# Weight pieces cut by half the columns instead of by rows, with five buffers for their split halves instead of six

## The chip, the cores and the metric

The kernel runs on one core of a Trainium2 chip. The metric is the device time of one execution in microseconds (us). TensorE multiplies matrices (PE in the profile), VectorE (DVE), ScalarE (ACT) and GpSimd (POOL) work element by element, and SyncE (SP) issues most of the DMAs. Each engine takes its own instructions strictly in the order in which they were written into its queue, and waits for semaphores in between.

## The reference

Two layers act on 512 tokens of 1024 values, each as `h = h + mixer(rms_norm(h)) @ w_out`, with an inner width of 2048. A last RMS norm closes it.

```python
def pool_mixer(h, w_in, w_grp, scale, w_out):          # layer 0
    v, gate = jnp.split(h @ w_in, 2, axis=-1)
    p = multiscale_pool(v)                              # 4 groups of 512, windows 2, 4, 8, 16
    m = jnp.einsum('btgc,gcd->btgd', p, w_grp).reshape(B, T, D_INNER) * scale
    return (m * jax.nn.silu(gate)) @ w_out

def hgrn2_mixer(h, w_in, lb, norm_g, w_out):            # layer 1, 16 heads of 128
    q, fz, i, gate = jnp.split(h @ w_in, 4, axis=-1)
    ...                                                 # forget gates, per head: S_t = diag(f_t) S_{t-1} + k_t v_t^T
    o = hgrn2_chunk_scan(qc, kc, vc, bc)                # o_t = S_t^T q_t
    o = o * lax.rsqrt(jnp.mean(o * o, axis=-1, keepdims=True) + EPS) * norm_g
    return (o * jax.nn.silu(gate)) @ w_out
```

## The kernel before

Activations lie with the features on the partitions, as tiles of 128 x 512 tokens. All large products are made from three fp32r matmuls (`mm3`, L127 to L130): a weight or activation `x` is split into `hi` (rounded by ACT, L96) and `lo = x - hi` (by DVE, L97), and the product is hi·hi + hi·lo + lo·hi. One such matmul has 512 columns.

Weights come in pieces of 128 x 1024 values (512 KB). For each piece `piece` (L99) takes a buffer `wraw` (three of them) for the DMA on SP's queue and a buffer each of `whi` and `wlo` (`WB`, six of each), issues the DMA, the ACT cast and the DVE subtraction, all with raised priority so that the scheduler places them early in the engines' queues. A cast waits until PE has made its last use of the piece that had the buffer before.

A group is 512 of the 2048 inner columns, four blocks of 128 (`n` = 0 to 3). `load_in` brings the 1024 x 512 weights of a group in four pieces of 256 rows each, so that every block `n` needs all four pieces: `project` (L142) runs over the eight row blocks `k` for one `n`. `load_out` brings the 512 x 1024 output weights in four pieces of 128 rows.

Layer 1 works on four groups of four heads. For group 1 to 3, `prepare` makes the forget gates (`forget`: the weights `wf`, then `fz`, the sigmoids `s1` on ACT, `f` and `kk` on DVE), a chain of twelve products along the chunk on `f` (L557, L558) for each pair of heads, and then `queries` (weights `wq`, `q`). From `f` POOL makes `r` (L571), DVE takes the reciprocal of `r` (L572, four in a group), and q and k are scaled by it. Then `inputs` (weights `wi`) makes `v` with the weights as the moving side: each of its blocks needs all four pieces, one after the other, from the first block on. After that come the attention of four heads, gates and `add_out`, which adds the output product to `ht` (tokens on the partitions, four blocks `b`, two halves of the columns).

`finish` (L505) makes the last output product. For each token block `b` it makes half 0 and half 1, adds each to `ht` (DVE, L379), squares them (ACT, L514), and then makes the factor of the norm (`ms` on DVE, L516 and L517, the power on POOL, L519) and the two outputs `y` (DVE, L523), which ACT and SP send away.

Tile and a priority scheduler set the order in each engine's queue; nothing is ordered by hand beyond `tc.high_priority`.

Of the kernel before, what the change touches and what calls it, by code (L numbers as in the profile page):

```python
# [32 lines left out]
F32 = mybir.dt.float32  # L33
# [7 lines left out]
P = 128  # L41
D = 1024
T = 512
DI = 2048
# [7 lines left out]
WINDOWS = (2, 4, 8, 16)  # L52
RAW, WB = 3, 6
WARM = 10
# [12 lines left out]
def trunk(ctx: ExitStack, tc: tile.TileContext, xT, x_d, par, ident_d, causal_d, mask_d, fg_d, w0_in, w0_grp, w0_out, w1_in, w1_out, out):  # L67
# [31 lines left out]
    def piece(src, ahead=AHEAD):  # L99

        raw = wpool.tile([P, 2, GC], F32, name="wraw", tag="wraw", bufs=RAW)
        hi = wpool.tile([P, 2, GC], F32R, name="whi", tag="whi", bufs=WB)
        lo = wpool.tile([P, 2, GC], F32R, name="wlo", tag="wlo", bufs=WB)
        with tc.high_priority(ahead):
            nc.sync.dma_start(out=raw, in_=src)
            split(raw, hi, lo)
        return hi, lo

    def load_in(w, col=0, ahead=AHEAD):
# [6 lines left out]
        return out  # L116

    def load_out(w, g):

        out = []  # L120
        for i in range(GT):
            r = g * GC + i * P
            hi, lo = piece(w[r:r + P, :].rearrange("p (a b) -> p a b", a=2))
            out.append((hi.rearrange("p a b -> p (a b)"), lo.rearrange("p a b -> p (a b)")))
        return out
# [20 lines left out]
    def project(pieces, n, xs, at=None):  # L146


        if at:
            acc = pa.tile([P, T], F32, name="a", tag="a", bufs=4)  # L150
        else:
            acc = ps.tile([P, T], F32, name="mm", tag="mm", bufs=4)
        c = slice(n * P, (n + 1) * P)
        for k, ((wh, wl), (xh, xl)) in enumerate(zip(pieces, xs)):
            if at and k in at:
                at[k]()
            mm3(acc, wh[:, c], wl[:, c], xh, xl, k == 0, k == len(pieces) - 1)
        return acc
# [60 lines left out]
    def project_out(pieces, zs):  # L219
        for n in range(KD):  # L220
            acc = project(pieces, n, zs)
            nc.vector.tensor_tensor(out=h[n], in0=acc, in1=h[n], op=ALU.add)  # L222


    with tc.tile_pool(name="l0", bufs=1) as l0:
# [20 lines left out]
        accs = project4(pieces, xs, None)  # L246
        wg0 = load_in(w0_in, DI, AHEAD0)
        norm = []
# [13 lines left out]
        def values(g):  # L262
            vs = []
            wv = None if g == 0 else load_in(w0_in, g * GC)
# [24 lines left out]
        def gates0(g):  # L289
            wg = wg0 if g == 0 else load_in(w0_in, DI + g * GC)  # L290
            out = []
# [11 lines left out]
        def mixed(g, ps_, gates):  # L303
            wm = load_in(w0_grp[g])
            out = []
# [43 lines left out]
    def hgrn(ctx, general):  # L349
# [23 lines left out]
        def out_half(pieces, zs, b, half):  # L373

            acc = ps.tile([P, 512], F32, name="mm", tag="mm", bufs=4)
            t, c = slice(b * P, (b + 1) * P), slice(half * 512, (half + 1) * 512)
            for k, ((wh, wl), (zh, zl)) in enumerate(zip(pieces, zs)):
                mm3(acc, zh[:, t], zl[:, t], wh[:, c], wl[:, c], k == 0, k == len(pieces) - 1)
            nc.vector.tensor_tensor(out=ht[b][:, c], in0=acc, in1=ht[b][:, c], op=ALU.add)  # L379

        def add_out(pieces, zs):
            for b in range(TB):
                for half in range(2):
                    out_half(pieces, zs, b, half)
# [10 lines left out]
        def forget(g, store):  # L395
            wf = None if g == 0 else load_in(w1_in, DI + g * GC)
            fs, ks = [], []
# [13 lines left out]
        def queries(g):  # L411
            wq = load_in(w1_in, g * GC)
            qs = []
# [63 lines left out]
        def group(g, prepare, heads, zs):  # L477
# [6 lines left out]
            if first or last:  # L484
                wg = load_in(w1_in, 3 * DI + g * GC)
                gts = gates1(wg, (0, 1))
                ons = [attend(n) for n in range(GT)]
                gts += gates1(wg, (2, 3))
            else:
                add_out(load_out(w1_out, g - 1), zs)  # L490
                ons = [attend(n) for n in range(GT)]
                gts = gates1(load_in(w1_in, 3 * DI + g * GC), range(GT))
            if first:
# [9 lines left out]
        def finish(zs):  # L503
# [3 lines left out]
            for i in range(2):  # L507
                nc.scalar.dma_start(out=fg[i], in_=fg_d[:, i * 512:(i + 1) * 512])
            for b in range(TB):
                ss = l1.tile([P, 2], F32, name="ss", tag="ss", bufs=2)  # L510
                for half in range(2):
                    out_half(wo, zs, b, half)
                    sq = small.tile([P, 512], F32, name="sq", tag="sq", bufs=2)
                    nc.scalar.activation(out=sq, in_=ht[b][:, half * 512:(half + 1) * 512], func=AF.Square, accum_out=ss[:, half:half + 1])  # L514
                ms = small.tile([P, 1], F32, name="ms", tag="ms", bufs=4)
# [4 lines left out]
                for half in range(2):  # L520
                    c = slice(half * 512, (half + 1) * 512)
                    y = act.tile([P, 512], F32, name="y", tag=f"x{'hl'[half]}{2 + b}", bufs=1)
                    nc.vector.scalar_tensor_tensor(out=y, in0=ht[b][:, c], scalar=rn, in1=fg[half], op0=ALU.mult, op1=ALU.mult)  # L523
                    (nc.sync if half else nc.scalar).dma_start(out=out[b * P:(b + 1) * P, c], in_=y)

        def factored():
# [286 lines left out]
```

## Time and profile before

| what | value |
|---|---|
| median of three runs | 828.61 us (828.05 to 829.05) |
| the profiled execution's own time | 828.94 us |
| its span, first to last instruction | 827.1 us |
| PE busy | 816.1 us (99%), 3902 matmuls |
| DVE busy | 546.2 us (66%) |
| ACT busy | 278.7 us (34%) |
| POOL busy | 150.3 us (18%) |
| granted TensorE clock | 0.997 of full speed |

The busy time of PE is a union of overlapping matmuls: each is shown with 0.39 us, and the next starts about 0.23 us after it. So a busy PE says that it is fed, and the distance of two starts says how fast. 1.8 us lie between the span and the time of the execution.

### The profile page before, as it was taken

What the parts mean: (1) busy time and instruction counts of PE and PEld (TensorE: products, weight loads), DVE (VectorE), ACT (ScalarE), POOL (GpSimd) and SP (SyncE); (2) the same over time, 40 slices, a digit from 0 to 9 for tenths busy, and PEclk for the clock granted to TensorE, in tenths of its full rate; (3) what the DMA queues carried; (4) which work ended last, traced back from release to release, by engine and by line L of the source; (5) the groups of instructions that cost most, each with busy time, mean ns of one, the idle gap of its engine ahead of it and who ended that gap; (6) DMA issues with size and microseconds to landing.
All of it is one profiled execution on the core that took longest, in us unless ns stands there. A gap on an engine that the chain in (4) does not pass through costs nothing.

```text
span 827.1 us, 10198 instructions
## 1 busy us (share of the span) xinstructions
PE 816.1 (99%) x3902; PEld 685.8 (83%) x3902; DVE 546.2 (66%) x837; ACT 278.7 (34%) x476; POOL 150.3 (18%) x197
## 2 busy tenths in 40 slices
PE   9999999999999999999999999999999999999995
PEld 8888888888888888888888888888888888888884
DVE  5687537854785465798169973359973459973744
ACT  7442134223234244325342241343240333242311
POOL 0030010002011032260313400313300313302100
PEclk9999999999999999999999999999999999999998
DMA  9531324223232155133033240333240333240302
GB/s 342 198 103 52 101 102 153 78 71 116 94 101 103 55 178 178 52 102 102 1 102 102 77 128 1 103 102 102 77 128 1 103 101 102 77 126 3 102 14 92
DMA packets 37769, 81.14 MB, mean 98 GB/s; under 512 B 2896, under 2 KB 3152, under 8 KB 37712
## 3 DMA queue, kind: packets, MB, share of 16 engines
q1 hardware_dynamic: 35264, 76.56, 28.3%
q10 hardware_dynamic: 2448, 3.86, 1.3%
q8 instruction: 32, 0.52, 0.3%
q14 instruction: 25, 0.20, 0.1%
HBM read 76.21 MB, written 4.19 MB: 97 GB/s over the span
## 4 chain that ended last, share of the span: by engine, by line
PE 95%; DVE 3%; issue 1%; DMA 0%; ACT 0%; POOLq 0%; POOL 0%; DVEq 0%; ACTq 0%
PE mm L128 29%; PE mm L129 28%; PE mm L130 28%; PE a L625 2%; PE a L627 1%; PE a L588 1%; PE a L605 1%; DVE r L572 1%; PE a L466 1%; DVE wlo L97 1%; PE a L83 1%; PE a L594 0%; DMA wraw<-in_w1i 0%; PE a L128 0%; PE a L130 0%
## 5 line engine op out<-in xcount | busy, mean ns | idle before, releaser
L128 PE MATMUL mm<-xh,whi 128*128 128x512 f32 x624 | 244.7, 392 | 0.0
L129 PE MATMUL mm<-xl,whi 128*128 128x512 f32 x624 | 243.2, 390 | 0.0
L130 PE MATMUL mm<-xh,wlo 128*128 128x512 f32 x624 | 243.0, 390 | 0.0
L96 ACT CAST whi<-wraw 128x1024 fp32r<-128x1024 f32 (+1 forms) x140 | 141.8, 1026 | 237.3 <-PE mm L129 108.6
L97 DVE TENSOR_TENSOR wlo<-wraw,whi 128x1024 fp32r<-128x1024 f32 (+1 forms) x140 | 172.0, 1253 | 56.6 <-ACT whi L96 54.5
L130 PEld LDWEIGHTS mm<-xh,wlo 128*128 128x128 f32 x624 | 117.3, 188 | 24.6
L128 PEld LDWEIGHTS mm<-xh,whi 128*128 128x128 f32 x624 | 117.4, 188 | 24.1 <-DVE h L222 0.3
L129 PEld LDWEIGHTS mm<-xl,whi 128*128 128x128 f32 x624 | 117.3, 188 | 24.2
L572 DVE RECIPROCAL r<-r 128x512 f32<-128x512 f32 x16 | 53.4, 3338 | 0.0
L128 PE MATMUL mm<-whi,xh 128*128 128x512 f32 x128 | 50.1, 391 | 0.0
L129 PE MATMUL mm<-wlo,xh 128*128 128x512 f32 x128 | 50.0, 391 | 0.0
L130 PE MATMUL mm<-whi,xl 128*128 128x512 f32 x128 | 49.9, 390 | 0.0
L129 PE MATMUL mm<-zl,whi 128*128 128x512 f32 x128 | 49.8, 389 | 0.0
L128 PE MATMUL mm<-zh,whi 128*128 128x512 f32 x128 | 49.8, 389 | 0.0
L130 PE MATMUL mm<-zh,wlo 128*128 128x512 f32 x128 | 49.8, 389 | 0.0
L379 DVE TENSOR_TENSOR ht<-mm,ht 128x512 f32<-128x512 f32 x32 | 22.0, 688 | 35.1 <-PE mm L130 35.1
L222 DVE TENSOR_TENSOR h<-mm,h 128x512 f32<-128x512 f32 x32 | 21.9, 688 | 28.4 <-PE mm L130 28.1
L442 POOL TENSOR_TENSOR gs<-fz,s 128x512 f32<-128x512 f32 x16 | 21.5, 1342 | 98.7 <-ACT s L440 98.7
L299 POOL TENSOR_TENSOR gs<-gt,sg 128x512 f32<-128x512 f32 x16 | 21.9, 1372 | 87.8 <-ACT sg L297 87.8
L128 PE MATMUL mm<-whi,z1h 128*128 128x512 f32 x96 | 37.6, 392 | 0.0
L130 PE MATMUL mm<-whi,z1l 128*128 128x512 f32 x96 | 37.4, 390 | 0.0
L129 PE MATMUL mm<-wlo,z1h 128*128 128x512 f32 x96 | 37.4, 389 | 0.0
(151 smaller groups left out, 1156.0 us busy)
## 6 DMA issues: line engine op xcount, KB each, us to landing
wraw<-in_w1i SPq DMA_DIRECT2D x64, 512.0 KB, 3.9
wraw<-in_w0i SPq DMA_DIRECT2D x28, 512.0 KB, 4.3
wraw<-in_w0o SPq DMA_DIRECT2D x16, 512.0 KB, 3.7
wraw<-in_w1o SPq DMA_DIRECT2D x16, 512.0 KB, 4.3
wraw<-in_w0g SPq DMA_DIRECT2D x8, 512.0 KB, 3.9
h<-in_xT SPq DMA_DIRECT2D x8, 256.0 KB, 5.1
wraw<-in_w0i SPq DMA_DIRECT2D x8, 256.0 KB, 5.3
xt<-in_x SPq DMA_DIRECT2D x4, 512.0 KB, 6.7
```

The lines of the kernel that those rows point to most:

```text
L83: nc.tensor.matmul(warm[:, :P], ones, ones, start=True, stop=True)
L96: nc.scalar.copy(out=hi, in_=src)
L97: nc.vector.tensor_tensor(out=lo, in0=src, in1=hi, op=ALU.subtract)
L128: nc.tensor.matmul(out, lh, rh, start=start, stop=False)
L129: nc.tensor.matmul(out, lh, rl, start=False, stop=False)
L130: nc.tensor.matmul(out, ll, rh, start=False, stop=stop)
L222: nc.vector.tensor_tensor(out=h[n], in0=acc, in1=h[n], op=ALU.add)
L299: nc.gpsimd.tensor_tensor(out=gs, in0=gt, in1=sg, op=ALU.mult)
L379: nc.vector.tensor_tensor(out=ht[b][:, c], in0=acc, in1=ht[b][:, c], op=ALU.add)
L442: nc.gpsimd.tensor_tensor(out=gs, in0=gt, in1=sg, op=ALU.mult)
L572: nc.vector.reciprocal(out=r, in_=r)
L625: nc.tensor.matmul(o[:, b], Ads[pr][:, j, t], v[:, b, n * P:(n + 1) * P], start=True, stop=b == 0)
```

## The change

`load_in` stays for the two loads that need all four blocks at once (the first one of layer 1, and `inputs`). All other input weights come through the new `load_cols`: four pieces again, but each is 512 rows by 256 columns, first the two pieces of the first 256 columns (blocks `n` = 0, 1), then the two of the second. `load_out` takes pieces of 256 rows by 512 columns, the first half of the columns first, and `add_out` and `finish` therefore run over the halves outside and the token blocks inside. `WB` goes from six to five. The number and the shapes of the matmuls, casts and subtractions stay the same.

```diff
-RAW, WB = 3, 6
+RAW, WB = 3, 5
...
+    def load_cols(w, col=0, ahead=AHEAD):
+        v = w.rearrange("(k p) n -> p k n", p=P)
+        out = []
+        for i in range(2):
+            cut = []
+            for k in range(0, v.shape[1], 4):
+                c = col + i * 256
+                hi, lo = (x.rearrange("p a (b c) -> p (a b) c", b=2) for x in piece(v[:, k:k + 4, c:c + 256], ahead))
+                cut += [(hi[:, j], lo[:, j]) for j in range(4)]
+            out += [[(hi[:, j * P:(j + 1) * P], lo[:, j * P:(j + 1) * P]) for hi, lo in cut] for j in range(2)]
+        return out
...
     def load_out(w, g):
+        v = w[g * GC:(g + 1) * GC, :].rearrange("(k p) n -> p k n", p=P)
         out = []
-        for i in range(GT):
-            r = g * GC + i * P
-            hi, lo = piece(w[r:r + P, :].rearrange("p (a b) -> p a b", a=2))
-            out.append((hi.rearrange("p a b -> p (a b)"), lo.rearrange("p a b -> p (a b)")))
+        for c in range(0, D, GC):
+            got = [piece(v[:, k:k + 2, c:c + GC]) for k in range(0, GT, 2)]
+            out.append([(hi[:, j], lo[:, j]) for hi, lo in got for j in range(2)])
...
         def add_out(pieces, zs):
-            for b in range(TB):
-                for half in range(2):
+            for half in range(2):
+                for b in range(TB):
                     out_half(pieces, zs, b, half)
...
         def finish(zs):
...
-            for b in range(TB):
-                ss = l1.tile([P, 2], F32, name="ss", tag="ss", bufs=2)
-                for half in range(2):
-                    out_half(wo, zs, b, half)
-                    sq = small.tile([P, 512], F32, name="sq", tag="sq", bufs=2)
-                    nc.scalar.activation(out=sq, in_=ht[b][:, half * 512:(half + 1) * 512], func=AF.Square, accum_out=ss[:, half:half + 1])
+            ss = l1.tile([P, TB, 2], F32, name="ss")
+
+            def scaled(b, ss):
                 ms = small.tile([P, 1], F32, name="ms", tag="ms", bufs=4)
...
+            for half in range(2):
+                c = slice(half * 512, (half + 1) * 512)
+                for b in range(TB):
+                    out_half(wo, zs, b, half)
+                    sq = small.tile([P, 512], F32, name="sq", tag="sq", bufs=2)
+                    nc.scalar.activation(out=sq, in_=ht[b][:, c], func=AF.Square, accum_out=ss[:, b, half:half + 1])
+                    if half:
+                        scaled(b, ss[:, b])
```

PE's own queue holds the same matmuls in the same places, but for three that change places with three others in layer 1's first load. What moves is the order on DVE and ACT. The lines of the changed kernel are some 14 to 20 higher: L393 is L379 of before, L402 is L388, L420 is L406, L432 is L418, L527, L528 and L534 are L516, L517 and L523, L566 is L546, L577 and L578 are L557 and L558, L592 is L572, and L596 and L597 are L576 and L577.

**First place.** DVE's queue in `prepare` of group 1, where the chain on the first pair's `f` (`f_3471`) ends; groups 2 and 3 have the same pattern. `wlo_3665` and `wlo_3671` are the third and fourth piece of `wq`, `wlo_3833` the first of `wi`, `fz_3608` and `kk_3546` are of the second pair of heads, and `r_3781` is the first head's. Before:

```order
L544 TENSOR_SCALAR f_3545<-s1_3574,lb_2442 128x4x64
L546 TENSOR_SCALAR first_3446<-s1_3574,lb_2442 128x4
L97 TENSOR_TENSOR wlo_3665<-wraw_3663,whi_3664 128x1024
L406 TENSOR_SCALAR kk_3546<-s1_3576,lb_2442 128x512
L97 TENSOR_TENSOR wlo_3671<-wraw_3669,whi_3670 128x1024
L97 TENSOR_TENSOR wlo_3833<-wraw_3831,whi_3832 128x1024
L388 TENSOR_TENSOR fz_3608<-mm_3583,rb_2642 128x512
L572 RECIPROCAL r_3781<-r_3781 128x512
```

In the changed kernel:

```order
L566 TENSOR_SCALAR first_3446<-s1_3574,lb_2442 128x4
L420 TENSOR_SCALAR kk_3546<-s1_3576,lb_2442 128x512
L577 TENSOR_TENSOR f_3471<-f_3471 128x8x32
L578 TENSOR_TENSOR f_3471<-f_3471 128x8x32
L97 TENSOR_TENSOR wlo_3671<-wraw_3669,whi_3670 128x1024
L592 RECIPROCAL r_3781<-r_3781 128x512
L97 TENSOR_TENSOR wlo_3833<-wraw_3831,whi_3832 128x1024
L402 TENSOR_TENSOR fz_3608<-mm_3583,rb_2642 128x512
```

The last two products of the chain stand behind the second pair's first `kk` now. The reciprocal follows them with one subtraction between, and the first `wi` piece and `fz_3608` are behind it instead of ahead. `wlo_3665` has left this place: it stands some twenty rows earlier, directly behind the second head's `fz` and ahead of that head's `f`.

**Second place.** The same queue further on, up to the fourth piece of `wi` (`wlo_3851`); `wlo_3845` is the third one, `r_3788` the second head's, `r_3795` the third's. Before:

```order
L572 RECIPROCAL r_3788<-r_3788 128x512
L418 TENSOR_TENSOR q_3728<-mm_3729,rb_2642 128x512
L576 TENSOR_TENSOR q_3675<-q_3675,r_3788 128x4x64
L577 TENSOR_TENSOR q_3675<-q_3675,f_3471 128x4x64
L572 RECIPROCAL r_3795<-r_3795 128x512
L97 TENSOR_TENSOR wlo_3845<-wraw_3843,whi_3844 128x1024
L97 TENSOR_TENSOR wlo_3851<-wraw_3849,whi_3850 128x1024
```

In the changed kernel:

```order
L432 TENSOR_TENSOR q_3728<-mm_3729,rb_2642 128x512
L596 TENSOR_TENSOR q_3675<-q_3675,r_3781 128x4x64
L597 TENSOR_TENSOR q_3675<-q_3675,f_3471 128x4x64
L596 TENSOR_TENSOR q_3675<-q_3675,r_3788 128x4x64
L597 TENSOR_TENSOR q_3675<-q_3675,f_3471 128x4x64
L592 RECIPROCAL r_3795<-r_3795 128x512
L97 TENSOR_TENSOR wlo_3851<-wraw_3849,whi_3850 128x1024
L97 TENSOR_TENSOR wlo_4062<-wraw_4060,whi_4061 128x1024
```

The second reciprocal has left this place; it stands directly behind `fz_3608`. `wlo_3845` has moved up as well, among the products on `f_3545`. The third reciprocal is still directly ahead of `wlo_3851`.

**Third place.** DVE's queue at the end of `finish`, token blocks 1 to 3. Before:

```order
L379 TENSOR_TENSOR ht2_2660<-mm_6632,ht2_2660 128x512
L516 TENSOR_TENSOR ms_6648<-ss_6615 128x1
L517 TENSOR_SCALAR ms_6648<-ms_6648 128x1
L523 SCALAR_TENSOR_TENSOR y_6653<-ht2_2660,rnf_6651,fg_6523 128x512
L523 SCALAR_TENSOR_TENSOR y_6656<-ht2_2660,rnf_6651,fg_6524 128x512
L379 TENSOR_TENSOR ht3_2661<-mm_6660,ht3_2661 128x512
L379 TENSOR_TENSOR ht3_2661<-mm_6676,ht3_2661 128x512
L516 TENSOR_TENSOR ms_6692<-ss_6659 128x1
```

In the changed kernel:

```order
L534 SCALAR_TENSOR_TENSOR y_6643<-ht1_2659,rnf_6638,fg_6524 128x512
L393 TENSOR_TENSOR ht2_2660<-mm_6646,ht2_2660 128x512
L527 TENSOR_TENSOR ms_6662<-ss_6527 128x1
L528 TENSOR_SCALAR ms_6662<-ms_6662 128x1
L393 TENSOR_TENSOR ht3_2661<-mm_6673,ht3_2661 128x512
L534 SCALAR_TENSOR_TENSOR y_6667<-ht2_2660,rnf_6665,fg_6523 128x512
L534 SCALAR_TENSOR_TENSOR y_6670<-ht2_2660,rnf_6665,fg_6524 128x512
L527 TENSOR_TENSOR ms_6689<-ss_6527 128x1
```

A token block has one sum left to add instead of two between the outputs of the block before and its own norm, and the last block's add stands ahead of the outputs of block 2, its norm behind them.

## Rows read from the trace of the kernel before

**Rows 1.** The page's busy time, share of the span and instructions of each engine.
```profile
PE 816.1 (99%) x3902; PEld 685.8 (83%) x3902; DVE 546.2 (66%) x837; ACT 278.7 (34%) x476; POOL 150.3 (18%) x197
```
**Rows 2.** The page's chain that ended last, share of the span by engine.
```profile
PE 95%; DVE 3%; issue 1%; DMA 0%; ACT 0%; POOLq 0%; POOL 0%; DVEq 0%; ACTq 0%
```
**Rows 3.** Waits of PE: engine, line, whom it waited for, us, times, longest.
```profile
PE a L594 <- ACT kt L596: 0.3, 1, 0.3
PE a L605 <- DVE Ad L591: 0.2, 1, 0.2
```
**Rows 4.** Timeline of PE, group 2, fourth piece of `wi`: start, us, instruction.
```profile
593.66 0.39 PE L128 MATMUL mm<-whi,xh 128*128 128x512 f32 x1
593.95 0.50 PE L129 MATMUL mm<-wlo,xh 128*128 128x512 f32 x1
```
**Rows 5.** Timeline of PE, group 1, the same place.
```profile
469.31 0.40 PE L129 MATMUL mm<-wlo,xh 128*128 128x512 f32 x1
```
**Rows 6.** Timeline of DVE, `prepare` of group 1.
```profile
433.09 0.41 DVE L543 TENSOR_SCALAR f<-s,lb 128x252 f32<-128x252 f32 x1 [0.76 <-ACT s L390]
...
434.33 0.42 DVE L557 TENSOR_TENSOR f<-f 128x256 f32<-128x256 f32 x1
...
438.28 0.42 DVE L557 TENSOR_TENSOR f<-f 128x256 f32<-128x256 f32 x1
438.62 0.42 DVE L558 TENSOR_TENSOR f<-f 128x256 f32<-128x256 f32 x1
...
446.01 3.33 DVE L572 RECIPROCAL r<-r 128x512 f32<-128x512 f32 x1
...
466.21 1.16 DVE L97 TENSOR_TENSOR wlo<-wraw,whi 128x1024 fp32r<-128x1024 f32 x1
...
467.29 1.75 DVE L97 TENSOR_TENSOR wlo<-wraw,whi 128x1024 fp32r<-128x1024 f32 x1
```
**Rows 7.** Timeline of POOL, `prepare` of group 1.
```profile
438.76 0.32 POOL L562 COPY ends<-f 128x8 f32<-128x8 f32 x1 [15.40 <-DVE f L557]
...
442.02 3.27 POOL L571 TENSOR_SCALAR r<-f 128x512 f32<-128x512 f32 x2
...
455.83 0.32 POOL L562 COPY ends<-f 128x8 f32<-128x8 f32 x1 [4.81 <-DVE f L557]
...
458.08 1.59 POOL L571 TENSOR_SCALAR r<-f 128x512 f32<-128x512 f32 x1
...
461.67 0.74 POOL L575 TENSOR_TENSOR kk<-kk,r 128x256 f32<-128x256 f32 x1 [2.00 <-DVE r L572]
...
466.38 1.58 POOL L575 TENSOR_TENSOR kk<-kk,r 128x256 f32<-128x256 f32 x1 [1.91 <-DVE r L572]
```
**Rows 8.** Timeline of DVE in `finish`.
```profile
806.85 0.69 DVE L379 TENSOR_TENSOR ht<-mm,ht 128x512 f32<-128x512 f32 x1 [0.87 <-PE mm L130]
808.39 0.16 DVE L516 TENSOR_TENSOR ms<-ss 128x1 f32<-128x1 f32 x1 [0.85 <-ACT sq L514]
...
809.40 1.41 DVE L523 SCALAR_TENSOR_TENSOR y<-ht,rnf,fg 128x512 f32<-128x512 f32 x2 [0.67 <-POOL rnf L519]
810.74 0.68 DVE L379 TENSOR_TENSOR ht<-mm,ht 128x512 f32<-128x512 f32 x1
...
817.73 0.69 DVE L379 TENSOR_TENSOR ht<-mm,ht 128x512 f32<-128x512 f32 x1 [0.82 <-PE mm L130]
...
820.34 1.41 DVE L523 SCALAR_TENSOR_TENSOR y<-ht,rnf,fg 128x512 f32<-128x512 f32 x2 [0.72 <-POOL rnf L519]
```
**Rows 9.** Timeline of DVE in group 0's `prepare`, and of ACT in its attention.
```profile
359.26 3.96 DVE L97 TENSOR_TENSOR wlo<-wraw,whi 128x1024 fp32r<-128x1024 f32 x3
...
382.76 1.04 ACT L96 CAST whi<-wraw 128x1024 fp32r<-128x1024 f32 x1 [1.68 <-DMA wraw<-in_w1i]
```
**Rows 10.** The page's DMA issues: count, KB each, us to landing.
```profile
wraw<-in_w1i SPq DMA_DIRECT2D x64, 512.0 KB, 3.9
wraw<-in_w1o SPq DMA_DIRECT2D x16, 512.0 KB, 4.3
```

More of the change, by code (lines that the diff above doesn't have):

```diff
@@ L104, in piece @@
         with tc.high_priority(ahead):
-            nc.sync.dma_start(out=raw, in_=src)
+            nc.sync.dma_start(out=raw if src.shape[1] == 2 else raw.rearrange("p a (b c) -> p (a b) c", b=2), in_=src)
             split(raw, hi, lo)
@@ L152, in project @@
             acc = ps.tile([P, T], F32, name="mm", tag="mm", bufs=4)
-        c = slice(n * P, (n + 1) * P)
-        for k, ((wh, wl), (xh, xl)) in enumerate(zip(pieces, xs)):
+        for k, ((wh, wl), (xh, xl)) in enumerate(zip(pieces[n], xs)):
             if at and k in at:
                 at[k]()
-            mm3(acc, wh[:, c], wl[:, c], xh, xl, k == 0, k == len(pieces) - 1)
+            mm3(acc, wh, wl, xh, xl, k == 0, k == len(xs) - 1)
         return acc
@@ L220, in project_out @@
         for n in range(KD):
-            acc = project(pieces, n, zs)
+            acc = project([[(hi[:, c:c + P], lo[:, c:c + P]) for hi, lo in half] for half in pieces for c in range(0, GC, P)], n, zs)
             nc.vector.tensor_tensor(out=h[n], in0=acc, in1=h[n], op=ALU.add)
@@ L246, in trunk @@
         accs = project4(pieces, xs, None)
-        wg0 = load_in(w0_in, DI, AHEAD0)
+        wg0 = load_cols(w0_in, DI, AHEAD0)
         norm = []
@@ L263, in values @@
             vs = []
-            wv = None if g == 0 else load_in(w0_in, g * GC)
+            wv = None if g == 0 else load_cols(w0_in, g * GC)
             for n in range(GT):
@@ L289, in gates0 @@
         def gates0(g):
-            wg = wg0 if g == 0 else load_in(w0_in, DI + g * GC)
+            wg = wg0 if g == 0 else load_cols(w0_in, DI + g * GC)
             out = []
@@ L303, in mixed @@
         def mixed(g, ps_, gates):
-            wm = load_in(w0_grp[g])
+            wm = load_cols(w0_grp[g])
             out = []
@@ L376, in out_half @@
             t, c = slice(b * P, (b + 1) * P), slice(half * 512, (half + 1) * 512)
-            for k, ((wh, wl), (zh, zl)) in enumerate(zip(pieces, zs)):
-                mm3(acc, zh[:, t], zl[:, t], wh[:, c], wl[:, c], k == 0, k == len(pieces) - 1)
+            for k, ((wh, wl), (zh, zl)) in enumerate(zip(pieces[half], zs)):
+                mm3(acc, zh[:, t], zl[:, t], wh, wl, k == 0, k == GT - 1)
             nc.vector.tensor_tensor(out=ht[b][:, c], in0=acc, in1=ht[b][:, c], op=ALU.add)
         def add_out(pieces, zs):
-            for b in range(TB):
-                for half in range(2):
+            for half in range(2):
+                for b in range(TB):
                     out_half(pieces, zs, b, half)
@@ L395, in forget @@
         def forget(g, store):
-            wf = None if g == 0 else load_in(w1_in, DI + g * GC)
+            wf = None if g == 0 else load_cols(w1_in, DI + g * GC)
             fs, ks = [], []
@@ L411, in queries @@
         def queries(g):
-            wq = load_in(w1_in, g * GC)
+            wq = load_cols(w1_in, g * GC)
             qs = []
@@ L484, in group @@
             if first or last:
-                wg = load_in(w1_in, 3 * DI + g * GC)
+                wg = load_cols(w1_in, 3 * DI + g * GC)
                 gts = gates1(wg, (0, 1))
@@ L491, in group @@
                 ons = [attend(n) for n in range(GT)]
-                gts = gates1(load_in(w1_in, 3 * DI + g * GC), range(GT))
+                gts = gates1(load_cols(w1_in, 3 * DI + g * GC), range(GT))
             if first:
```

## The prediction

> **What bounds the kernel now.** I read the page's busy times first: PE is busy 99% of the span [rows 1]. Busy alone proves little, since matmuls overlap, so the chain that ended last comes next: 95% of it is PE, 3% DVE [rows 2]. Then PE's waits: behind the start there are two, of 0.3 and 0.2 us, both in group 0's attention [rows 3]. Last, the timeline of PE, for stalls too short for that view. A matmul starts about 0.23 us after the one before; in group 2 one starts 0.29 us after, where the subtraction of the last `wi` piece was only just done [rows 4], and its successor lost another 0.1. In group 1 that subtraction ends at 469.04 (467.29 plus 1.75) and PE wants it at 469.31 [rows 5, 6]. The reader is to see that PE runs at its pace nearly throughout, that all its stalls together are about 0.7 us, and that behind the last matmul there is a tail: the last add starts at 817.73 and the span ends at 827.1 [rows 8]. A change that leaves the matmuls alone can win 0.7 us in the middle. It can lose much more, in the middle and at the tail.
>
> **The change part by part.** The matmuls, casts, subtractions and bytes are as many as before, so I count only what moves.
>
> *Pieces by columns, five buffers.* With `load_cols` a block needs two pieces of four. The tightest buffer is that of the last `wi` piece in each `prepare`: it comes from the third `wq` piece, which PE leaves 12 matmuls ahead of the end of `wq`, and it is wanted 18 matmuls into `wi`. That is 30 matmuls at 0.23 us and some transposes, about 8 us, the same as before with six buffers, where the piece came free at the same matmul. All other pieces behind the start have more than half a load, 11 us (48 matmuls), between. A cast and a subtraction take 1.04 and 1.16 us [rows 6, 9]. So buffers cost nothing, as long as DVE comes to the subtraction in time; what that costs if it does not is the third term.
>
> *Shorter runs in the DMAs.* `load_cols` reads runs of 1 KB where `load_in` reads 2 KB. No row shows 1 KB runs of this size. The nearest: 512 KB in 4 KB runs (`in_w1o`) took 4.3 us to landing and in 2 KB runs (`in_w1i`) 3.9 [rows 10], so halving the run cost nothing there. Below I take 0, above another 3.9 us if the time were to double. By the Trainium skill (DMA: Bandwidth & Descriptors, "Why small descriptors are slow") each packet carries about three fixed cycles, which speaks against this change; an estimate from its 32-byte beats, 2 x 35 against 67, gives 4% or 0.2 us a piece, and the sum would be 0.2 us higher. The trace's 2 KB and 4 KB rows do not show such a cost. Only one wait on a landing lies near PE's path, in group 0: the cast at 382.76 waited for it [rows 9]. I take 0.
>
> *Group 0's attention, -0.5 us.* Both waits of rows 3 hang behind that cast: the ACT copies and the DVE masks stand in the queues behind it and its subtraction. Its DMA waited for a raw buffer, which an earlier subtraction frees. Three subtractions of 3.96 us together stood between the first two reciprocals of group 0 [rows 9]. In the new order two of the subtractions and the fourth `q` go ahead of the first reciprocal, in part where DVE was idle, so what follows comes somewhat earlier. Bounds: nothing, and both waits, 0.6 us with rounding. I take 0.5, since half a microsecond of lead is enough to cover them.
>
> *The reciprocals in groups 1 to 3, +1.8 us.* This is the disputed term. I walk DVE's queue in group 1.
> 1. The third `wq` piece's subtraction now stands ahead of the second head's gate. DVE waited 0.76 us there [rows 6]; the rest of the 1.16 us and the wait for the cast push on by about 0.7. That is made good by two products of the chain on `f` (0.34 each, 438.28 to 438.62) that no longer stand ahead of the next `fz`.
> 2. But these two products now stand behind that head's gate: 1.24 us (433.09 to 434.33) plus 0.67. So the product for which POOL waits starts at 440.26, where it started at 438.28: 2.0 later.
> 3. POOL then starts at 440.74 instead of 438.76 [rows 7]. From there to the first `r` it took 4.9 us (442.02 plus half of 3.27, less 438.76) beside DVE's subtractions, and 3.84 us in the later run (458.08 plus 1.59, less 455.83). So the first `r` is there at 444.6 to 445.7; I take 445.0, as DVE is mostly idle meanwhile.
> 4. DVE comes to the reciprocal at about 442.3 and waits, with all behind it. It started at 446.01 before, so it starts 1.0 earlier now. But the first `wi` piece (1.16 to 1.6) and the fourth `fz` (0.6) stood ahead of it and stand behind it now.
> 5. From that reciprocal to the fourth `wi` piece it was 21.28 us (446.01 to 467.29); now 21.28 + 1.3 + 0.6 = 23.2, and 0.3 more because the third reciprocal follows closely on the POOL instruction that makes its `r`. That puts the subtraction at 468.5. It takes 1.16 if it gets ahead of POOL's L575 as at 466.21, and 1.75 if it falls behind it as at 467.29 [rows 6, 7]. It ends at 469.7 to 470.3, PE wants it at 469.31 [rows 5], with some 0.1 us for the semaphore: a stall of 0.5 to 1.1. I take 0.6, near the lower end, since the subtraction is the first behind its reciprocal, as the one at 466.21 was.
>
> The bounds of a group: with `r` at 444.6, no POOL wait and 1.16 it ends at 468.8, no stall; with 445.7, 1.6 and 1.75 at 471.2, a stall of 2.0. Three times 0.6 is 1.8. The 0.15 us that PE loses in group 2 today goes away with the old order, so 1.65 net. What is queued behind the waiting reciprocal (`fz`, `q`) has a spare PSUM buffer, and PE does not wait for it.
>
> On 0.6 against more: by the Trainium skill (SBUF — State Buffer, "Who interferes with whom") a GpSimd instruction and a DVE instruction with two SBUF inputs lock each other out, the one that starts first goes through. By that rule the subtraction would take 1.16 us if it starts first and up to 1.9 if second (1.16 plus the 0.74 that L575 takes alone), which makes the stall 0.5 or 1.2 and the sum 831.4 or 833.5; the trace agrees, with 1.16 and 1.75 in rows 6 beside L575.
>
> *The tail, +1.9 us.* In `finish` PE makes the second halves one after the other, 2.72 us apart (four adds from 806.85 to 817.73). For each, DVE's queue holds add, norm, two outputs, and the next add behind them. Add to next add is 3.89 us (806.85 to 810.74), of which ACT's square and POOL's power are waiting [rows 8]. Before, a row block had 5.44 us, so this was hidden; now it falls behind PE. Adds start at 809.57 (817.73 less 3 x 2.72), 813.46 and 817.35. Block 2's norm ends 1.9 later, at 819.2 (1.54 to 808.39, and two short operations), then comes the last add (0.7), then block 2's two outputs, to 821.24 (1.34 from 819.9). The last norm could start 1.54 behind the last add, at 820.8, but its place is behind those outputs. The last outputs start 1.01 after it (808.39 to 809.40), at 822.25, against 820.34: 1.9. Every part has its row, so I hold it to 0.3 either way. The outputs' DMAs follow as before.
>
> **Sum.** 828.94 (the profiled execution; its span is 827.1) - 0.5 + 1.65 + 1.9 = 832.0. That execution lies 0.33 above the median of 828.61, so I forecast **831.7 us**.
>
> **The rivals.**
> - *Tail alone.* The fourth `wi` piece is in time (step 5's lower end), as DVE wins in groups 1 to 3 what step 2 loses. For it: the first reciprocal starts a microsecond earlier than before, and 0.6 is a small difference of large sums. Against it: the wait for POOL, and two operations more behind that reciprocal. 828.61 - 0.65 + 1.9 = 829.9, +0.15%.
> - *Not slower.* DVE keeps up with PE in `finish`, and with the last `wi` pieces as well; then the tail is as long as today and the stalls of today go: 828.61 - 0.65 = 828.0. The point from which it decides is a distance of add to add of 2.72 us or less. For it: DVE is busy only 66% of the span [rows 1]. Against it: the 3.89 us measured with the same operations in the same order [rows 8].
> - *More in the middle.* Steps 3 and 5 at their upper ends, 2.0 us a group: 828.61 - 0.65 + 6.0 + 1.9 = 835.9. For it: L575's 1.75; against: an idle DVE leaves POOL undisturbed.
> - *DMA the bound.* 1 KB runs take twice as long: group 0's cast comes 3 us later, 831.7 + 0.5 + 2.5 = 834.7 or so. Against: rows 10.
>
> **How the numbers follow.** The forecast, 830.3 to 833.5, gets 0.47; tail alone 0.25; not slower 0.11; more in the middle 0.10; DMA 0.07. From 829.0 to 834.8 takes in the forecast, most of tail alone and part of the higher cases, a little over 8 in 10. About 0.2% (1.66 us) is what a measurement of this kernel can tell from no change; faster by that means under 826.95, which no case reaches, and I leave 0.05 for what I have not seen. Same, 826.95 to 830.27, has tail alone and not slower, 0.31; slower 0.64.
>
> **What the changed profile would show.** PE's waits name the subtraction, once in each of groups 1 to 3, some 0.6 us; DVE is idle 2 to 3 us ahead of each group's first reciprocal, released by POOL; the two waits of group 0 are gone or shorter; in `finish` the adds of the last three blocks stand 3.9 us apart, and the last output starts about 4.5 us behind PE's end, not 2.6. The forecast is wrong if POOL's `r` is there before DVE asks, if the last `wi` subtraction ends before PE's request, or if any other load shows a wait for a landing.

## The result and the profile after

The changed kernel takes **834.66 us** (median of 4 runs, 834.19 to 835.26), the one before 828.38 (828.05 to 829.05): 1.0076 times as long, 95% interval 1.006 to 1.0092. That is slower, as forecast, but by 6.3 us where 3.1 were forecast, and at the upper edge of the stated range.

The page after: busy times and the chain that ended last, beside [rows 1, 2].

```profile
span 833.5 us, 10212 instructions
PE 817.3 (98%) x3902; PEld 685.9 (82%) x3902; DVE 545.1 (65%) x837; ACT 282.4 (34%) x476; POOL 157.2 (19%) x197
PE 80%; DVE 11%; issue 3%; POOL 3%; DMA 2%; ACT 1%; POOLq 0%; DVEq 0%; ACTq 0%
wraw<-in_w1i SPq DMA_DIRECT2D x64, 512.0 KB, 3.7
```

The work is the same, but PE's share of the chain has gone from 95% to 80%: from each new wait of PE the chain runs back through DVE and POOL. PE's waits behind the start in the changed kernel, beside [rows 3]:

```profile
PE mm L144 <- DVE wlo L97: 2.6, 3, 0.9
PE a L614 <- ACT kt L616: 0.7, 2, 0.4
PE a L625 <- DVE Ad L611: 0.5, 2, 0.2
```

Three waits for a subtraction, one in each of groups 1 to 3, are new. The attention waits (L614, L625) were once in group 0; now there is a second set in group 1. This view counts only idle time, so I take the sizes from the starts of the matmuls. PE's timeline in group 1:

```profile
468.75 0.39 PE L143 MATMUL mm<-whi,xh 128*128 128x512 f32 x1
470.02 0.50 PE L144 MATMUL mm<-wlo,xh 128*128 128x512 f32 x1 [0.88 <-DVE wlo L97]
470.35 0.39 PE L145 MATMUL mm<-whi,xl 128*128 128x512 f32 x1
```

470.02 less 468.75 is 1.27, where the pace is 0.23, and the next matmul is 0.10 late: a stall of 1.15. The same start-to-start reading over the whole run gives where the 6.4 us between the two spans (833.5 and 827.1) went:

| stretch | us |
|---|---|
| start to the end of group 0's attention | -0.35 |
| fourth `wi` piece, groups 1 to 3: 3 x 1.15, less 0.19 that group 2 lost before | +3.25 |
| attention waits, group 1 | +1.27 |
| attention waits, group 3 | +0.3 |
| last matmul to last outputs | +2.0 |

(6.47 in all. The last row goes to the start of the last outputs; from the last matmul to the span's end it is 1.94 more, which gives the 6.4.)

Now DVE in group 1 (idle time ahead of an instruction and its releaser in brackets), beside [rows 6]:

```profile
440.40 1.22 DVE L97 TENSOR_TENSOR wlo<-wraw,whi 128x1024 fp32r<-128x1024 f32 x1
444.86 3.35 DVE L592 RECIPROCAL r<-r 128x512 f32<-128x512 f32 x1 [3.25 <-POOL r L591]
...
465.53 3.35 DVE L592 RECIPROCAL r<-r 128x512 f32<-128x512 f32 x1 [1.39 <-POOL r L591]
468.80 2.83 DVE L97 TENSOR_TENSOR wlo<-wraw,whi 128x1024 fp32r<-128x1024 f32 x2
```

and POOL, beside [rows 7]:

```profile
440.21 1.46 POOL L582 COPY ends<-f 128x8 f32<-128x8 f32 x1 [16.96 <-DVE f L577]
...
443.34 2.94 POOL L591 TENSOR_SCALAR r<-f 128x512 f32<-128x512 f32 x2
...
460.74 0.32 POOL L582 COPY ends<-f 128x8 f32<-128x8 f32 x1 [6.76 <-DVE f L577]
...
463.23 3.72 POOL L591 TENSOR_SCALAR r<-f 128x512 f32<-128x512 f32 x2 [0.47 <-DVE q L596]
```

DVE waits 3.25 us ahead of the first reciprocal and 1.39 ahead of the third, and directly behind the third stands the subtraction that PE wants at 468.98 (468.75 and the pace of 0.23). POOL's copy L582 takes 1.46 us; at 460.74 in the same group it takes 0.32. The 1.46 end at 441.67, when DVE's subtraction beside it ends (441.62). With the rule of the Trainium skill (SBUF — State Buffer, "Who interferes with whom") that a DVE instruction with two SBUF inputs and a GpSimd instruction that reads SBUF lock each other out, this trace agrees.

The tail, DVE in `finish`, beside [rows 8]:

```profile
817.92 0.68 DVE L393 TENSOR_TENSOR ht<-mm,ht 128x512 f32<-128x512 f32 x1
820.47 1.41 DVE L534 SCALAR_TENSOR_TENSOR y<-ht,rnf,fg 128x512 f32<-128x512 f32 x2 [0.67 <-POOL rnf L530]
821.81 0.68 DVE L393 TENSOR_TENSOR ht<-mm,ht 128x512 f32<-128x512 f32 x1
823.60 0.68 DVE L393 TENSOR_TENSOR ht<-mm,ht 128x512 f32<-128x512 f32 x1
...
826.79 1.42 DVE L534 SCALAR_TENSOR_TENSOR y<-ht,rnf,fg 128x512 f32<-128x512 f32 x2 [0.72 <-POOL rnf L530]
```

Add to add is 3.89 us (817.92 to 821.81), as the prediction had it. PE's last matmul, before and then in the changed kernel:

```profile
817.31 0.39 PE L130 MATMUL mm<-whi,zz 128*128 128x512 f32 x1
```

```profile
821.77 0.39 PE L145 MATMUL mm<-whi,zz 128*128 128x512 f32 x1
```

So the last outputs start 5.02 us behind it (826.79), against 3.03 before (820.34 in [rows 8]).

### The profile page after: what moved, and what is told of

The parts are those of the page before. It is cut to its first block, busy times and chain, and to the rows that moved or that the text cites. A ratio compares the mean times of both kernels' runs of the same rounds, so it can differ in the third digit from the quotient of the medians.

```text
span 833.5 us, 10212 instructions
## 1 busy us (share of the span) xinstructions
PE 817.3 (98%) x3902; PEld 685.9 (82%) x3902; DVE 545.1 (65%) x837; ACT 282.4 (34%) x476; POOL 157.2 (19%) x197
## 4 chain that ended last, share of the span: by engine, by line
PE 80%; DVE 11%; issue 3%; POOL 3%; DMA 2%; ACT 1%; POOLq 0%; DVEq 0%; ACTq 0%
PE mm L144 24%; PE mm L143 24%; PE mm L145 24%; DVE wlo L97 3%; DVE r L592 3%; PE a L645 2%; POOL r L591 1%; PE a L647 1%; PE a L625 1%; DMA wraw<-in_w1i 1%; DVE q L432 1%; DVE f L577 1%; DVE f L578 1%; DVE y L534 1%; ACT whi L96 1%
## 5 line engine op out<-in xcount | busy, mean ns | idle before, releaser
L97 DVE TENSOR_TENSOR wlo<-wraw,whi 128x1024 fp32r<-128x1024 f32 (+1 forms) x140 | 168.5, 1207 | 97.3 <-ACT whi L96 95.4
L96 ACT CAST whi<-wraw 128x1024 fp32r<-128x1024 f32 (+1 forms) x140 | 144.0, 1028 | 255.3 <-PE mm L144 180.1
L144 PEld LDWEIGHTS mm<-xl,whi 128*128 128x128 f32 x624 | 117.3, 188 | 23.9
L592 DVE RECIPROCAL r<-r 128x512 f32<-128x512 f32 x16 | 53.5, 3345 | 13.9 <-POOL r L591 13.9
L456 POOL TENSOR_TENSOR gs<-fz,s 128x512 f32<-128x512 f32 x16 | 26.4, 1651 | 97.9 <-ACT s L454 97.9
L313 POOL TENSOR_TENSOR gs<-gt,sg 128x512 f32<-128x512 f32 x16 | 24.4, 1526 | 89.6 <-ACT sg L311 89.6
L393 DVE TENSOR_TENSOR ht<-mm,ht 128x512 f32<-128x512 f32 x32 | 22.0, 688 | 28.5 <-PE mm L145 28.5
L468 POOL TENSOR_TENSOR ro<-mo,mhalf 128x4 f32<-128x4 f32 x16 | 16.2, 1015 | 101.0 <-DVE mo L466 101.0
```

The costliest lines, as they stand in the source:

```text
L96: nc.scalar.copy(out=hi, in_=src)
L97: nc.vector.tensor_tensor(out=lo, in0=src, in1=hi, op=ALU.subtract)
L144: nc.tensor.matmul(out, lh, rl, start=False, stop=False)
L313: nc.gpsimd.tensor_tensor(out=gs, in0=gt, in1=sg, op=ALU.mult)
L456: nc.gpsimd.tensor_tensor(out=gs, in0=gt, in1=sg, op=ALU.mult)
L468: nc.gpsimd.tensor_tensor(out=ro[:, :, 0], in0=mo, in1=mhalf[:, :TB], op=ALU.pow)
```

## The experiments

Each kernel was timed against the kernel before on the same chip (medians of 828.25 to 828.37 us). Behind a median stand its lowest and highest run, then its ratio to the kernel before with a 95% interval.

**Buffers.** The forecast gave them nothing. The first run puts the sixth back into the changed kernel, the second takes it from the kernel before.

```diff
-RAW, WB = 3, 5
+RAW, WB = 3, 6
```

> The changed kernel with six buffers for halves instead of five (834.7 us changed, 828.4 before). The order of VectorE in the four groups is unchanged by it, only layer 0 is ordered anew. Theory A (five buffers cost: in group 1 a piece of w_out gets its buffer only at 483, its subtraction frees the raw buffer at 486, the next piece's load lands at 491, and PE waits 1.1 us for attention copies and masks queued behind that piece's cast and subtraction; 0.2 us in group 3): these waits go, the three waits of 1.15 us for the last wi subtraction stay, the tail stays: 833.3 us. Theory B (the prediction's: buffers cost nothing, the attention waits come from the late subtraction ahead of them or from the shorter runs): 834.7, the waits at 492 to 494 stay.

Measured: 832.45 us (831.66 to 832.92), 1.0047 (1.0033 to 1.0061). Neither theory holds as written: the time fell by 2.2 us, but it was the three `wi` waits that went, and the attention waits of groups 0 and 1 that stayed (the 0.3 us of group 3 went too). PE's waits and DVE around the third reciprocal:

```profile
PE a L614 <- ACT kt L616: 1.0, 2, 0.7
PE mm L144 <- DVE pl L97: 0.7, 1, 0.7
...
466.38 3.35 DVE L592 RECIPROCAL r<-r 128x512 f32<-128x512 f32 x1 [1.38 <-POOL r L591]
469.65 2.83 DVE L97 TENSOR_TENSOR wlo<-wraw,whi 128x1024 fp32r<-128x1024 f32 x2
```

The reciprocal waits just as long (1.38), and two subtractions stand behind it as before. But they are not the same pieces. DVE's queue with its names, changed kernel and six buffers:

```
L592 RECIPROCAL r_3795<-r_3795 128x512
L97 TENSOR_TENSOR wlo_3851<-wraw_3849,whi_3850 128x1024
L97 TENSOR_TENSOR wlo_4062<-wraw_4060,whi_4061 128x1024

L592 RECIPROCAL r_3795<-r_3795 128x512
L97 TENSOR_TENSOR wlo_4062<-wraw_4060,whi_4061 128x1024
L97 TENSOR_TENSOR wlo_4068<-wraw_4066,whi_4067 128x1024
```

The places for subtractions in the order stay; with a buffer more every piece moves one place ahead. The fourth `wi` piece (`wlo_3851`) then has the place ahead of the third reciprocal and is done at 459.85, 10 us early. The piece that is left behind the reciprocal is one of `w_out`, wanted 26 us later. Behind layer 0 the traced execution is 3.5 us shorter than the changed kernel's: in layer 0 it has a wait of 0.7 us for `pl` more. That wait also shows in the next but one kernel below, whose layer 0 is the changed kernel's, so not the buffers alone make it, and how often the timed executions have it is not known.

> The kernel before with five buffers instead of six, all else as before (828.4 us). Theory A: attention waits of about 1 us appear in groups 1 to 3 or some of them, behind a cast whose load came late, 829.5 to 831. Theory B (buffers cost nothing): 828.4, within 0.3 us. Either way no change in the tail, since finish is as before.

Measured: 832.22 us (831.82 to 832.5), 1.0047 (1.0033 to 1.0061). Five buffers alone cost the kernel before 4.0 us. Theory B is refuted, and A again named the wrong waits: what appears are `wi` waits.

```profile
PE mm L129 <- DVE wlo L97: 2.1, 3, 0.7
...
462.52 3.34 DVE L572 RECIPROCAL r<-r 128x512 f32<-128x512 f32 x1
465.79 3.96 DVE L97 TENSOR_TENSOR wlo<-wraw,whi 128x1024 fp32r<-128x1024 f32 x3
...
465.92 0.39 PE L128 MATMUL mm<-whi,xh 128*128 128x512 f32 x1
467.00 0.50 PE L129 MATMUL mm<-wlo,xh 128*128 128x512 f32 x1 [0.69 <-DVE wlo L97]
```

In the kernel before, the three subtractions from 466.21 on [rows 6] are the third and fourth `wi` piece and one of `w_out`; with five buffers they are the second, third and fourth `wi`. The second is wanted at 466.15 and comes 0.85 late. So in both kernels five buffers move the pieces one place back. With column pieces they stand two places further ahead than with row pieces, at five buffers as at six; what makes the place behind the third reciprocal late in the changed kernel all the same is that this reciprocal starts at 465.53 there and at 462.52 here.

**The waiting reciprocal.** The other half of the same stall, by taking away what DVE waits for.

```diff
-                        nc.gpsimd.tensor_scalar(out=r, in0=fs[pr][:, j], scalar1=FLOOR, scalar2=None, op0=ALU.max)
+                        nc.vector.tensor_scalar(out=r, in0=fs[pr][:, j], scalar1=FLOOR, scalar2=None, op0=ALU.max)
```

> The changed kernel, but the maximum that makes r ahead of each reciprocal runs on VectorE instead of GpSimd (16 instructions of about 0.6 us moved). Theory A (the last wi subtraction is late because VectorE waits 3.25 us ahead of the first and 1.4 us ahead of the third reciprocal of a group for GpSimd's r): the first reciprocal starts 2 us earlier, the last wi subtraction ends near 468.3 where PE wants it at 469.0, the three waits of 1.15 us go, 831.2 us. Rival (VectorE's own work fills the time, the wait hides nothing): it gets 0.6 us more work per reciprocal, the waits grow, 835 to 837.

Measured: 832.15 us (831.65 to 833.54), 1.0046 (1.0032 to 1.006). The three `wi` waits are gone, with the fourth piece still behind the third reciprocal:

```profile
443.33 0.76 DVE L591 TENSOR_SCALAR r<-f 128x512 f32<-128x512 f32 x2
444.00 3.35 DVE L592 RECIPROCAL r<-r 128x512 f32<-128x512 f32 x1
...
463.86 3.35 DVE L592 RECIPROCAL r<-r 128x512 f32<-128x512 f32 x1
467.12 2.84 DVE L97 TENSOR_TENSOR wlo<-wraw,whi 128x1024 fp32r<-128x1024 f32 x2
...
PE a L614 <- DVE Ad L611: 1.0, 1, 1.0
```

The third reciprocal starts 1.7 us earlier, though PE is 1.8 us later there than in the changed kernel. About 1.6 us of that came back in group 0, where DVE's masks are now late (last line), so 2.5 us were won by the medians, not 3.45. In the changed kernel the stall needs both: a late third reciprocal and the fourth piece behind it.

**The tail.** Three runs. In the first the norm and outputs of a block are written behind the next block's add.

```diff
-                    if half:
-                        scaled(b, ss[:, b])
+                    if half and b:
+                        scaled(b - 1, ss[:, b - 1])
+            scaled(TB - 1, ss[:, TB - 1])
```

> The changed kernel, but in finish the norm and outputs of a block are issued behind the add of the next block, so that no add waits for the norm of the block before. If the tail costs 1.9 us because add to next add takes 3.89 us: adds 2.72 us apart, last output starts 2.6 us behind the last matmul, 832.8 us. Rival (the last outputs are bound by their transfers or by the late subtractions): 834.7.

Measured: 835.04 us (834.46 to 835.16), no gain. The edit did not do what it says:

```profile
819.46 0.75 DVE L534 SCALAR_TENSOR_TENSOR y<-ht,rnf,fg 128x512 f32<-128x512 f32 x1 [0.67 <-POOL rnf L530]
820.13 0.68 DVE L393 TENSOR_TENSOR ht<-mm,ht 128x512 f32<-128x512 f32 x1
...
823.39 0.69 DVE L393 TENSOR_TENSOR ht<-mm,ht 128x512 f32<-128x512 f32 x1
```

The scheduler puts one output of the block before ahead of the add all the same, so adds still wait for a norm (3.26 us apart). It says nothing against the tail theory. The other two runs do what they say: the changed kernel with the blocks outside in `finish`, and the kernel before with only `finish` and its `w_out` load in halves.

```diff
-            for half in range(2):
-                c = slice(half * 512, (half + 1) * 512)
-                for b in range(TB):
+            for b in range(TB):
+                for half in range(2):
+                    c = slice(half * 512, (half + 1) * 512)
                     out_half(wo, zs, b, half)
...
-                    if half:
-                        scaled(b, ss[:, b])
+                scaled(b, ss[:, b])
```

> The changed kernel (834.7 us), but finish takes the row blocks one after the other again, both halves of each, so that 5.44 us lie between two norms. Pieces, buffers and all ahead of finish are as changed. If the tail costs 1.9 us by the adds behind the norms: last output starts 2.6 us behind the last matmul instead of 4.6, 832.8 us. Rival (what kept the version with the late norm from being faster is the transfers of the outputs, not VectorE's queue): 834.7.

```diff
-            wo = load_out(w1_out, NG - 1)
+            wo = out_cols(w1_out, NG - 1)
...
-            for b in range(TB):
-                ss = l1.tile([P, 2], F32, name="ss", tag="ss", bufs=2)
-                for half in range(2):
-                    out_half(wo, zs, b, half)
...
+            for half in range(2):
+                c = slice(half * 512, (half + 1) * 512)
+                for b in range(TB):
+                    out_cols_half(wo, zs, b, half)
```

> The kernel before (828.3 us, six buffers, pieces by rows), and only finish and its last load of w_out by column halves, first half first. Tail theory: adds of the last three blocks 3.9 us apart, last output starts 4.6 us behind the last matmul, 830.2 us, and no wait in the middle is new. Rival (the tail grows only because the middle is late): 828.3.

Measured: 833.23 us (832.56 to 833.29), 1.0054 (1.004 to 1.0068), and 830.06 (829.88 to 830.7), 1.0023 (1.0014 to 1.0032). First PE's last matmul and the last outputs with blocks outside, then the same of before with halves:

```profile
821.62 0.39 PE L145 MATMUL mm<-whi,zz 128*128 128x512 f32 x1
...
824.66 1.42 DVE L534 SCALAR_TENSOR_TENSOR y<-ht,rnf,fg 128x512 f32<-128x512 f32 x2 [0.72 <-POOL rnf L530]
```

```profile
816.38 0.39 PE L139 MATMUL mm<-whi,zz 128*128 128x512 f32 x1
...
821.41 1.41 DVE L537 SCALAR_TENSOR_TENSOR y<-ht,rnf,fg 128x512 f32<-128x512 f32 x2 [0.72 <-POOL rnf L533]
```

3.04 us with blocks outside, 5.03 with halves outside: 2.0 us in the trace, 1.4 and 1.7 in the medians. The order of the loops in `finish` alone makes the tail.

**The attention waits.** In group 1 the masks and copies stand behind the cast of the first gate piece, which waits for its load; that load waits for a raw buffer until 486.08. Two runs: a fourth raw buffer, and the same gate load in row pieces (2 KB runs).

```diff
-RAW, WB = 3, 5
+RAW, WB = 4, 5
```

> The changed kernel with four buffers for the raw loads instead of three, still five for halves. Theory (PE waits in the attention of groups 0, 1 and 3 because the load ahead of the masks can start only when the subtraction three pieces before it is done, at 486.1 in group 1, and lands 3.7 to 5.2 us later): that load starts a piece earlier and has long landed, the attention waits go, all three waits for the last wi subtraction stay, 833 us. Rival (the attention waits come from VectorE's masks being late in themselves): the waits stay, 834.7.

Measured: 833.09 us (832.56 to 833.2), 1.0055 (1.0042 to 1.0069), 1.6 us less. ACT in the changed kernel, and with four raw buffers:

```profile
491.29 1.04 ACT L96 CAST whi<-wraw 128x1024 fp32r<-128x1024 f32 x1 [1.78 <-DMA wraw<-in_w1i]
```

```profile
486.57 1.05 ACT L96 CAST whi<-wraw 128x1024 fp32r<-128x1024 f32 x1 [0.30 <-PE mm L145]
...
PE mm L144 <- DVE wlo L97: 2.6, 3, 0.9
...
PE a L614 <- DVE Ad L611: 0.3, 1, 0.3
```

The cast no longer waits for a load, the waits in groups 1 and 3 are gone, in group 0 0.3 us is left, and the `wi` waits stand as they were (2.6). Group 0's attention is now 0.65 us shorter than in the kernel before, by the starts of the matmuls: the fourth raw buffer takes away a wait there that the change had not made.

```diff
-                gts = gates1(load_cols(w1_in, 3 * DI + g * GC), range(GT))
+                gts = gates1(load_rows(w1_in, 3 * DI + g * GC), range(GT))
```

> The changed kernel, with the gate weights of groups 1 and 2 loaded in row pieces (runs of 2 KB) instead of column pieces (1 KB). The first of them is the load that came late in group 1. Theory 1 (a shorter run makes this load slow, 5.2 us from free buffer to cast against 3.7 with rows): 3.7 us, the wait of 1.1 us in group 1's attention goes, 833.5 us, unless row pieces with five buffers bring new waits in the gates. Theory 2 (it is late by something else): 4.3 to 5.5 us as in the four runs of column pieces, the wait stays.

Measured: 834.17 us (833.9 to 834.43), 1.007 (1.0056 to 1.0083), 0.5 us less. The load took 4.57 us, which lies in the range of Theory 2, and group 1's wait is still there, 0.63 us long by the starts of the matmuls. In five traces with column pieces and three raw buffers the load took 4.3 to 5.5 us (four of them 5.2 and more) and the wait was 0.4 us in the trace with 4.3 and 1.3 to 1.5 in the others, so the run does not show that row pieces help. The load of the same kind in group 2 took 3.7 in each of the five, so the length of the runs does not explain the late one either.

The DMA view shows one thing that the theories left out. While the load of group 1 is under way (486.1 to 491.3 in the changed kernel), one packet of 16 KB on the queue that the profile calls instruction shares the 16 DMA engines with it:

```profile
q8 instruction: 1, 0.02, 1.4%
```

1.4% of 16 engines over 5.2 us is 1.2 us of one engine. All five traces and the one with row pieces have such a packet there. Where it took 1.0 us the load took 4.3, with 1.2 it took 5.2, with 1.9 to 2.0 it took 5.4 to 5.5 (with row pieces: 1.3 and 4.57). No such packet lies in the load of group 2 in the five, nor in this load in the kernel before (3.75 us), where it comes behind the landing. That makes it the likely cause, but no run moved the packet, so it is not shown.

**All three undone.** Four raw buffers, the maximum on DVE in groups 1 to 3, `finish` by blocks; column pieces and five buffers stay.

```diff
-RAW, WB = 3, 5
+RAW, WB = 4, 5
...
-                        nc.gpsimd.tensor_scalar(out=r, in0=fs[pr][:, j], scalar1=FLOOR, scalar2=None, op0=ALU.max)
+                        (nc.vector if g else nc.gpsimd).tensor_scalar(out=r, in0=fs[pr][:, j], scalar1=FLOOR, scalar2=None, op0=ALU.max)
```

> The changed kernel with column pieces and five buffers kept, and each of the three costs undone at once: four raw buffers (attention waits), the maximum ahead of the reciprocals on VectorE in groups 1 to 3 (waits for the last wi subtraction), finish by row blocks (tail). If the three add up: 834.7 less 1.6, less 3.45, less 1.6 to 1.9 gives 827.7 to 828.1, no wait of PE over 0.4 us behind group 0, last output 2.65 us behind the last matmul, the time of the kernel before (828.3) or a little under. Rival (undoing one brings back another, as the maximum on VectorE did in group 0): 829 to 831.

Measured: **827.26 us** (826.83 to 827.8, 11 runs), 0.9988 (0.9979 to 0.9997): faster than both kernels. Behind the start PE waits once:

```profile
PE a L613 <- DVE Ad L610: 0.3, 1, 0.3
```

So the three causes make up the whole loss, and 1.0 us more is won. By the starts of the matmuls 0.65 of that lies in group 0's attention, as with four raw buffers alone, 0.2 in group 2 (the stall of [rows 4]) and 0.1 in layer 1's first load. The kernel before was not run with four raw buffers, so whether the column pieces are worth anything is not shown.

Two further runs shorten the tail, in this kernel and in the one before, by multiplying with the final gain beside the square:

```diff
+                    wf = small.tile([P, 512], F32, name="wf", tag="hg", bufs=2)
+                    nc.vector.tensor_tensor(out=wf, in0=ht[b][:, c], in1=fg[half], op=ALU.mult)
...
-                    nc.vector.scalar_tensor_tensor(out=y, in0=ht[b][:, c], scalar=rn, in1=fg[half], op0=ALU.mult, op1=ALU.mult)
+                    if half:
+                        nc.vector.tensor_scalar(out=y, in0=ws[b][half], scalar1=rn, scalar2=None, op0=ALU.mult)
+                    else:
+                        nc.scalar.activation(out=y, in_=ws[b][half], func=AF.Copy, scale=rn)
```

> As the kernel with the three costs undone, and in finish the product with the final gain is made beside the square, so that behind the norm only a scaling by one number per row is left, half on ScalarE and half on VectorE. The two outputs of the last block took 1.41 us one after the other behind the norm; in parallel some 0.7 us: 0.7 to 0.8 us less than that kernel, 827.0 to 827.3, so 0.1% to 0.17% under the kernel before. Rival (the end of the span is the landing of a transfer issued by the other queue, or ScalarE's scaling is slower than VectorE's two outputs): no gain.

> The kernel before, and only its finish with the product beside the square as in the kernel with the short tail. 828.3 less 0.7 to 0.8: 827.5 to 827.7. Rival (transfers bind the end): 828.3. If this is as fast as the kernel with the three costs undone and the short tail, the column pieces are worth nothing even without their costs.

Measured: 827.35 us (826.72 to 827.6), 0.9987 (0.9978 to 0.9996), and 828.16 (827.82 to 828.91), 1.0 (0.9991 to 1.0009). No gain in either. The last output's issue without the short tail, and then with it:

```profile
819.25 0.34 ACTq L535 DMA_DIRECT2D out_y<-y  x1
...
819.91 0.33 SPq L535 DMA_DIRECT2D out_y<-y  x1
```

```profile
819.92 0.34 ACTq L538 DMA_DIRECT2D out_y<-y  x1
...
819.68 0.33 SPq L538 DMA_DIRECT2D out_y<-y  x1
```

Against PE's last matmul (815.43 and 816.19) the last issue comes 0.75 us earlier, as meant. But both transfers now start almost together, and from the last issue to the span's end it is 5.9 us (825.8) where it was 5.3 (825.2). The difference lies in the landing of the transfer issued last, first without the short tail, then with it (us from issue to landing at the end):

```profile
out_y<-y SPq DMA_DIRECT2D x1, 256.0 KB, 3.0
```

```profile
out_y<-y ACTq DMA_DIRECT2D x1, 256.0 KB, 3.6
```

In both the span ends 2.3 us behind that landing. So 0.6 of the 0.75 is given back, and what is left is less than the medians can tell.

## Why the prediction was right in sign and half in size

The forecast's sum was +3.05 us and the traces show 6.4. About half of what was missing is the size of one term (the reciprocals, 1.6), the other half a wait that the sum did not have (attention in groups 1 and 3, 1.6). The time lies above the forecast's own case (830.3 to 833.5), and only 0.14 us inside the range that was stated round it.

- *Buffers, 0: wrong, and the step that failed first.* The forecast compared when a buffer comes free with when PE wants it, and found the last `wi` piece at the same matmul as before. That was true, but it asked the wrong question: with one buffer fewer each piece takes the place of its successor in DVE's queue, and the place behind the third reciprocal is late. Five buffers cost 4.0 us with row pieces, and with column pieces 2.2 by the medians, 3.5 by the traces behind layer 0. This is no cost beside the next term: with column pieces it is the same three waits. The forecast priced the fourth piece's late place there, and did not see that the fifth buffer had put it there.
- *The reciprocals, +1.65: mechanism right, the size half.* Each step came out within 0.6 us: POOL starts at 440.21 (forecast 440.74), `r` is there at 444.86 (445.0), the fourth subtraction starts at 468.80 (468.5). It ends at 469.96, inside the forecast 469.7 to 470.3. The third reciprocal waits 1.39 us for its `r`, where 0.3 was counted: POOL starts on that `r` only when DVE's product with the first `r`, which had the same buffer, is done (463.23, released by L596). In the kernel before the second reciprocal stood between that product and the third reciprocal, so POOL's time did not show. But from the first reciprocal to the subtraction it is 23.9 us, where 23.5 were forecast, so only 0.4 of that wait counts. The larger part is that PE came 0.33 earlier than before: the sum took 0.5 off ahead of this place and still let PE want the piece at 469.31. And I took 0.6 from a range of 0.5 to 1.1. It is 1.15 a group, 3.25 net.
- *Group 0, -0.5: wrong.* Its two waits lost only 0.1 us. The load ahead of them is issued when a subtraction ends at 378.55 (378.87 before); that subtraction's own cast waits for PE at 375.04, and then a reciprocal and the two products on `q` behind it hold DVE to 377.34. Moving other subtractions ahead of the first reciprocal did not move this one.
- *What the forecast did not have: the same attention wait in groups 1 and 3, 1.3 and 0.3.* A load that came 1.5 us later than its like in the kernel before (5.21 against 3.75) was enough. By the forecast's own sign, any other load that shows a wait for a landing, it was wrong here. More raw buffers remove the wait; that row pieces shorten it is not shown. The 0.3 of group 3 is also gone in three runs that leave the raw buffers at three, and its cause is open.
- *The tail, +1.9: right* (2.0 in the trace, 1.4 to 1.7 by medians).
- *The rivals.* "More in the middle" was nearest by its mechanism: 835.9 by 2.0 us a group; the middle did lose more, but over two mechanisms. "DMA the bound" has the nearest number, 834.7, by chance: it is refuted as put, since the `in_w1i` loads did not take twice as long. They landed in a median of 3.7 us (page above), all in 2 KB runs in 3.9 [rows 10]. By the Trainium skill (DMA: Bandwidth & Descriptors, "Why small descriptors are slow") shorter packets carry relatively more fixed cost. The traces can't tell whether these do: in the changed kernel the 44 loads in 1 KB runs have a median of 3.8 and the 20 in 2 KB runs 3.6, but all of the 44 overlap another load and half of the 20 do not.

## What to carry to other kernels

Where a scheduler fixes the order of an engine's queue, the number of buffers decides not only when a transfer may start but which piece stands at which place: follow the piece PE wants next to its place in the queue, and look at what is slow ahead of it. Counting the slack of each buffer by PE alone finds no stall that is made on another engine. When a loop is turned so that short rounds replace long ones at the end of a kernel, compare a round of the engine behind PE with PE's: here 3.89 us against 2.72.

## What the runs showed of the hardware that was not expected

- One load of 512 KB in group 1 took 4.3 to 5.5 us from free buffer to cast in five kernels, its like in group 2 3.7 in all of them. The first shared the DMA engines with one 16 KB packet of the instruction queue, the second did not; the longer the packet took (1.0 to 2.0 us), the longer the load. That the packet is the cause is not shown.
- Of two output transfers of 256 KB issued 0.24 us apart on two queues the later one landed 3.6 us behind its issue, of two issued 0.66 apart 3.0.
